# A hybrid convolution and Hyena encoder layer: channel-major inverse transforms, one 31-tap convolution for both groups, stored low parts of weights

## The chip, the cores and the metric

One core of a Trainium2 chip. The metric is the device time of one execution in microseconds. Engines are named as in the profile: PE (TensorE), DVE (VectorE), ACT (ScalarE), POOL (GpSimd), SP (SyncE, which here issues the DMAs).

## What is computed

One encoder layer is applied with the same weights to two groups of tokens, gp (512) and gs (1024), with 1024 features:

```python
h = _ln(x) * (1.0 + scale1) + shift1
proj = jnp.einsum('bld,de->ble', h, w_in)            # 4608 columns, 36 chunks of 128
a = a_val * jax.nn.sigmoid(a_gate)
a = _dwconv(a, conv_dw_w, conv_dw_b)                 # 31 taps, 512 channels
a = jax.nn.silu(_ln(a, conv_ln_g, conv_ln_b))
u = _dwconv(hy_in, hy_short_w, hy_short_b)           # 3 taps, 1536 channels: v, x1, x2
zb = x1 * _fftconv(v, filt[:, 0], hy_skip[0])        # circular, length 2L
zb = x2 * _fftconv(zb, filt[:, 1], hy_skip[1])
m = jax.nn.sigmoid(g_a) * (a @ conv_pw_w) + jax.nn.sigmoid(g_b) * (zb @ hy_out_w)
x = _ln(DEEPNORM_ALPHA * x + gate1 * (m @ w_out), ln1_g[l], ln1_b[l])
f = jnp.square(jax.nn.relu(h2 @ mlp_w1 + mlp_b1)) @ mlp_w2 + mlp_b2
x = _ln(DEEPNORM_ALPHA * x + gate2 * f, ln2_g[l], ln2_b[l])
```

scale, shift and gate come from a product of c with w_ada; filt is the transform of filters that a small MLP with sines makes (`filter_mlp`, `filters`).

## The kernel before

All large products are made of three f32r matmuls. A weight piece (`wpiece`, L209) is loaded into a raw buffer (4 of them), ACT copies it into wt[:, 0] at reduced width (the high part), and DVE subtracts that from raw into wt[:, 1] (the low part); there are six wt buffers. `mm3` (L223) then multiplies high by high, high by low and low by high. Activations are split in the same way into pg tiles. Every instruction on DVE and PE is issued through a `Meter` (L137), whose helper line, 145, stands in the trace for all of them; 202 is the copy in `split`.

The main line runs in this order: w_in(gp), w_in(gs), branches(gp) with the weights w_y, w_out(gp) with the first LayerNorm, the MLP of gp, branches(gs), w_out(gs), and the two products of gs's MLP (`up_seven`, `down_seven`). In the trace these begin at about 38, 270, 905, 960, 1027, 1389, 1502 and 1590 us, up to 2350. w_in takes 36 chunks of 128 columns, two weight pieces each, for 512 tokens at a time; the results go to DRAM as d_a (conv branch), d_h (Hyena) and d_g (gates).

Beside the main line runs side work, in generators that stop at each `yield`: the filters, a Hyena block of 128 channels (`hyena`, four per group), the 31-tap convolution of 128 channels (`conv31`), and its LayerNorm (`conv_ln`). Two lists of them, the lanes, get shares by LANES (L30). After each piece of the main line `pump` (L1623) issues side work as long as the DVE cost counted so far (`vector_cost`, divided by SHARE) is below the PE cost (`tensor_cost`). These costs thus set where side instructions stand between the main ones; each engine then executes its own list in order. Side work of gp that is left when w_in(gs) ends is finished there; that of gs runs on through w_y(gp), w_out(gp) and the MLP of gp.

A Hyena block transforms 128 channels: three-tap convolution (`conv3`), transpose to tokens (`to_tokens`), forward matmuls against tables (fx<-fp,fft), product with the spectrum of the filter (ks, on DVE as sg<-fx,sg), inverse matmuls (`inv_mm`, L355), and sums in `inv_bfly`. It does this twice. The first inverse is token-major (fx<-sg,fft: tables as weights, four matmuls of 128 columns per tile), so that its result meets x1 transposed; the second is channel-major (fx<-fft,sg: the spectrum as weights, two matmuls of 256 columns per tile). In an order's names the tables' tile is fft, PSUM tiles are fx, mm and tr. `conv31` pads one group's 128 channels by 15 on each side and adds 30 shifted products on DVE (cv<-cv,pp, 512 or 1024 columns) to ACT's first.

All DMAs that are named here stand in SP's queue, in order.

Of the kernel before, what the change touches and what calls it, by code (L numbers as in the profile page):

```python
# [25 lines left out]
TAPS = 31  # L26
# [3 lines left out]
LANES = (0.65, 0.35)  # L30
SHARE = 0.88
# [13 lines left out]
STEPS = 3  # L45
PS = (4, 3, 1)
# [14 lines left out]
def fft_tables():  # L61


    n = np.arange(128)[:, None].astype(np.float64)
    k = np.arange(128)[None, :].astype(np.float64)
    h = k[:, :64]
    c0, s0 = np.cos(2 * np.pi * n * h / 128), np.sin(2 * np.pi * n * h / 128)
    s0[:, 0] = (-1.0) ** np.arange(128)
    c8, s8 = np.cos(2 * np.pi * n * (h + 0.5) / 128), np.sin(2 * np.pi * n * (h + 0.5) / 128)
    first = [np.hstack([c0, c8]), np.hstack([c0, -c8]), np.hstack([s0, s8]), np.hstack([s0, -s8])]  # L70
    w = np.ones((64, 1))
    w[0] = 0.5
# [81 lines left out]
def vector_cost(args):  # L154
    return 0.065 + max(free_size(x) for x in args[:2]) / 960.0


def tensor_cost(args):
    return free_size(args[0]) * args[0].shape[0] / 128.0 * (0.00167 if args[2].dtype == F32 else 0.000417)


class Enc:
# [135 lines left out]
    def fwd_mm(self, ti, ev, q, ps):  # L298
# [12 lines left out]
        else:  # L311
            o = self.fft0 + 3 * (ti - 1)
# [42 lines left out]
    def inv_mm(self, g, ys, chan_major):  # L355

        nc, t, f = self.nc, self.T, self.fft
        outs = []
        for pr, y in enumerate(ys):
# [1470 lines left out]
```

## Time and profile before

| | |
|---|---|
| median of 3 runs | 2347.53 us (2347.05 to 2348.93) |
| profiled execution | 2351.76 us, its span 2350.0 us |
| granted TensorE clock, mean | 0.993 |
| busy: PE, DVE, ACT | 2267.9, 1890.1, 920.5 us |
| HBM | 316.16 MB read, 94.43 MB written |

Busy time says how long an engine had an instruction in execution; neighbours overlap by a little, so that counts times durations exceed it. PE's rows are passes: an f32 matmul shows as two rows, an f32r one as one. The span is divided into stretches below, and within a stretch the engine to look at is the one whose instructions the others wait for.

### The profile page before, as it was taken

The numbers are of one execution on the slowest core, as the hardware profiler recorded it, in microseconds if no ns is written. First come the engines' busy times: TensorE is split into PE (matmuls) and PEld (weight loads), VectorE is DVE, ScalarE is ACT, GpSimd is POOL, SyncE is SP. The second block draws the span as 40 slices with busy tenths as digits, with TensorE's granted clock in tenths as the row PEclk, the third lists the DMA queues.
The fourth block names the chain that finished last, engine by engine and source line by source line (L and its number), as shares of the span: only waits on it lengthen the run. The fifth ranks groups of instructions, "written<-read, shape, count | busy, mean of one in ns | idle before, by whom it ended". The sixth has DMA issues, their size and how long they took to land.

```text
span 2350.0 us, 33224 instructions
## 1 busy us (share of the span) xinstructions
PE 2267.9 (97%) x11684; PEld 1882.4 (80%) x11684; DVE 1890.1 (80%) x3662; ACT 920.5 (39%) x1521; POOL 54.3 (2%) x149
## 2 busy tenths in 40 slices
PE   6999999999999999989999999999999999999998
PEld 3878777778878888978888888789887777788886
DVE  5989797786989998895898875965987777577888
ACT  3464522422232223356543344222574444444430
POOL 2210100000000000000000000000000000000000
PEclk9999999999999999999999999999999999999999
DMA  6555434564356646634443344653675666876631
GB/s 246 179 169 175 138 113 163 195 224 159 133 188 203 200 174 215 218 116 144 144 135 99 94 157 154 210 156 109 210 247 188 215 205 214 283 241 215 205 124 71
DMA packets 201068, 412.80 MB, mean 176 GB/s; under 512 B 23321, under 2 KB 33739, under 8 KB 200389
## 3 DMA queue, kind: packets, MB, share of 16 engines
q1 hardware_dynamic: 200069, 409.67, 53.0%
q8 instruction: 92, 1.51, 0.3%
q0 software_dynamic: 832, 1.02, 0.2%
q14 instruction: 75, 0.61, 0.1%
HBM read 316.16 MB, written 94.43 MB: 175 GB/s over the span
## 4 chain that ended last, share of the span: by engine, by line
PE 79%; DVE 9%; DMA 8%; ACT 2%; issue 2%; SPq 1%; DVEq 0%; ACTq 0%
PE mm L145 57%; PE fx L145 19%; PE tr L145 3%; DVE sg L145 2%; DVE pg L145 2%; DVE wt L145 1%; DMA fp<-in_dec_s_dram 1%; DMA sg<-d_xs 1%; DMA fp<-in_w_ada_dram 1%; DVE st L145 1%; DVE fp L145 1%; DMA sg<-in_ffn_w_dram 1%; DMA sg<-ks 1%; DMA raw<-in_w_out_dram 1%; DVE xt L145 1%
## 5 line engine op out<-in xcount | busy, mean ns | idle before, releaser
L145 PE MATMUL mm<-pg,wt 128*128 128x512 f32 (+1 forms) x4776 | 1139.7, 391 | 5.0 <-DVE xt L145 3.6
L145 PEld LDWEIGHTS mm<-pg,wt 128*128 128x128 f32 x4776 | 878.7, 189 | 194.4 <-issue 11.9
L145 PE MATMUL mm<-wt,pg 128*128 128x512 f32 (+1 forms) x2556 | 480.8, 344 | 9.5 <-DVE wt L145 5.0
L145 PEld LDWEIGHTS mm<-wt,pg 128*128 128x128 f32 x2556 | 404.8, 190 | 68.6 <-DVE wt L145 6.8
L202 ACT ACTIVATE wt<-raw 128x512 fp32r<-128x512 f32 x430 | 268.7, 630 | 476.1 <-PE mm L145 375.7
L145 DVE TENSOR_TENSOR wt<-raw,wt 128x512 fp32r<-128x512 f32 x430 | 290.2, 684 | 80.0 <-ACT wt L202 78.1
L145 DVE SCALAR_TENSOR_TENSOR cv<-cv,pp 128x512 f32<-128x512 f32 (+1 forms) x288 | 288.7, 1009 | 7.3 <-ACT cv L853 2.3
L145 PEld LDWEIGHTS fx<-fp,fft 128*128 128x128 f32 x1536 | 177.5, 192 | 20.2 <-issue 15.1
L145 PE MATMUL fx<-fp,fft 128*128 128x128 f32 x1536 | 184.1, 277 | 1.7 <-DVE sm L145 1.1
L145 DVE TENSOR_TENSOR fp<-fp 128x256 f32<-128x256 f32 (+2 forms) x328 | 145.0, 481 | 15.6 <-ACT fp L380 10.2
L145 DVE TENSOR_TENSOR sg<-fx,sg 128x512 f32<-128x512 f32 (+1 forms) x162 | 98.6, 629 | 43.9 <-PE fx L145 27.7
L145 DVE TENSOR_TENSOR pg<-so,pg 128x512 fp32r<-128x512 f32 (+1 forms) x162 | 99.6, 623 | 38.3 <-ACT pg L202 26.9
L145 PE MATMUL fx<-pg,pg 128*128 128x512 f32 x492 | 120.7, 394 | 7.2 <-ACT pg L202 4.3
L145 PEld LDWEIGHTS fx<-pg,pg 128*128 128x128 f32 x492 | 93.5, 190 | 27.5 <-ACT pg L202 4.7
L202 ACT ACTIVATE pg<-so 128x512 fp32r<-128x512 f32 (+1 forms) x127 | 72.1, 575 | 73.9 <-DVE so L145 52.0
L145 PE MATMUL fx<-wt,pg 128*128 128x512 f32 x387 | 95.5, 389 | 0.0
L1260 ACT ACTIVATE so<-so,pp 128x512 f32<-128x512 f32 x62 | 44.4, 719 | 128.8 <-DVE so L145 128.7
L145 DVE TENSOR_TENSOR sg<-sg 128x256 f32<-128x256 f32 (+2 forms) x187 | 82.3, 460 | 6.4 <-ACT sg L890 5.0
L145 PEld LDWEIGHTS fx<-wt,pg 128*128 128x128 f32 x387 | 72.7, 188 | 15.1
L145 PE MATMUL mm<-pg,pg 128*128 128x512 f32 x300 | 73.9, 396 | 5.5 <-DVE xt L145 5.5
L380 ACT ACTIVATE fp<-fx 128x512 f32<-128x512 f32 x48 | 28.7, 598 | 120.6 <-PE fx L145 110.4
L145 DVE TENSOR_TENSOR pg<-pg,pg 128x1024 fp32r<-128x1024 f32 (+1 forms) x45 | 55.0, 1221 | 24.4 <-ACT pg L202 19.6
(175 smaller groups left out, 2221.4 us busy)
## 6 DMA issues: line engine op xcount, KB each, us to landing
raw<-in_mlp_w_dram SPq DMA_DIRECT2D x232, 256.0 KB
raw<-in_w_in_dram SPq DMA_DIRECT2D x144, 256.0 KB
xr<-in_mlp_w_dram SPq DMA_DIRECT2D x104, 256.0 KB
fp<-in_w_ada_dram SPq DMA_DIRECT2D x48, 512.0 KB
pg<-d_p SPq DMA_DIRECT2D x44, 512.0 KB
raw<-in_w_out_dram SPq DMA_DIRECT2D x64, 256.0 KB
d_p<-so SPq DMA_DIRECT2D x64, 256.0 KB
d_g<-so SPq DMA_DIRECT2D x48, 256.0 KB
```

Source lines behind the costliest of these rows:

```text
L145: return f(*args, **kw)
L202: self.nc.scalar.activation(hi, src, AF.Copy)
L380: nc.scalar.activation(outs[-1][:, 4 * (pr % 2):4 * (pr % 2) + 4].rearrange("p (j w) c -> p j w c", j=2), ps, AF.Copy)
L1260: nc.scalar.activation(out, src, AF.Relu, bias=self.pp[:, C_B1 + f:C_B1 + f + 1], scale=1.0)
```

## The change

Three things are changed, and the numbers that place the side work.

- `inv_mm` makes both inverses channel-major with new tables. A real spectrum's inverse is split into the part that is even and the part that is odd about the middle of a block, 64 columns each; two matmuls of 128 columns per tile, instead of four of 128 or two of 256, give the sums, and `unfold` makes the 128 values of a block from them on DVE (a sum, and a difference written backwards). The first inverse's result is therefore channel-major, is multiplied by x1 without a transpose, and is itself transposed for the second transform. The tables fft_sig have 41 blocks of 128 x 128 (2624 KB) where fft_sym had 29 (1856 KB).
- `conv31` takes both groups side by side in one tile (512 + 30 + 1024 columns), in w_in(gs). Its LayerNorm follows for both.
- Chunks 13 to 36 of gp's order in w_in (KEEP = 12) store their low part in DRAM (d_wl); w_in(gs) loads it into the wt buffer in place of the subtraction on DVE.
- LANES, SHARE and the cost functions have other numbers.

```diff
-LANES = (0.65, 0.35)
-SHARE = 0.88
+LANES = (0.4, 0.6)
+SHARE = 1.0
+KEEP = 12
 def vector_cost(args):
-    return 0.065 + max(free_size(x) for x in args[:2]) / 960.0
+    return 0.146 + max(free_size(x) for x in args[:2]) / 960.0
 def tensor_cost(args):
-    return free_size(args[0]) * args[0].shape[0] / 128.0 * (0.00167 if args[2].dtype == F32 else 0.000417)
+    return free_size(args[0]) * args[0].shape[0] / 128.0 * (0.00175 if args[2].dtype == F32 else 0.000443)
-    def inv_mm(self, g, ys, chan_major):
+    def inv_mm(self, g, ys):
...
-                if chan_major:
-                    p = ps[:, j].rearrange("p a b -> p (a b)")
-                    t.matmul(p, yr, f[:, mr[0]:mr[0] + 2].rearrange("p a b -> p (a b)"), start=True, stop=False)
-                    t.matmul(p, yi, f[:, mi[0]:mi[0] + 2].rearrange("p a b -> p (a b)"), start=False, stop=True)
-                else:
-                    for w in range(2):
-                        t.matmul(ps[:, j, w], f[:, mr[w]], yr, start=True, stop=False)
-                        t.matmul(ps[:, j, w], f[:, mi[w]], yi, start=False, stop=True)
+                p = ps[:, j].rearrange("p w (h n) -> p (w h) n", h=2)
+                for n, to in enumerate((slice(0, 3, 2), slice(1, 4, 2)) if ti == 0 else (slice(0, 4, 3), slice(1, 3))):
+                    self.T.matmul(p[:, to], y[:, j, n], f[:, 25 + 2 * ti + n], start=True, stop=True)
...
+    def unfold(self, g, e, mul):
+        v = self.V
+        y = self.fp()
+        a, b = e[:, 0:g.nt, 0:64], e[:, 0:g.nt, 64:128]
+        v.tensor_tensor(y[:, 0:g.nt, 0:64], a, b, op=ALU.add)
+        v.tensor_tensor(y[:, 0:g.nt, 127:63:-1], a, b, op=ALU.subtract)
+        v.tensor_tensor(y[:, 0:g.nt], y[:, 0:g.nt], mul, op=ALU.mult)
+        return y
...
-        dst = self.fp()
-        v.tensor_tensor(dst, e, mul, op=ALU.mult)
-        return dst
+        return self.unfold(g, e, mul)
...
+    def w_in_piece(self, g, c, i):
+        src = self.a["w_in"][c, i]
+        if g.r == 0 or c not in self.keep:
+            return self.wpiece(src, (128, 4, 128))
+        nc = self.nc
+        with self.soon(HW):
+            raw = self.p_raw.tile([128, 4, 128], F32, tag="raw", name="raw")
+            nc.sync.dma_start(raw, src)
+            w = self.p_wt.tile([128, 2, 4, 128], F32R, tag="wt", name="wt")
+            nc.sync.dma_start(w[:, 1].bitcast(F32), self.d_wl[c, i])
+            nc.scalar.activation(w[:, 0], raw, AF.Copy)
+        return w
+    def w_in_pieces(self, g, c):
+        ws = [self.w_in_piece(g, c, i) for i in range(2)]
+        if g.r == 0 and c in self.keep:
+            for i in range(2):
+                self.nc.sync.dma_start(self.d_wl[c, i], ws[i][:, 1].bitcast(F32))
+        return ws
...
+    def hyena(self, g, c):
+        z = blocks(self.conv3(g, c))
+        for o in range(2):
+            x = self.to_tokens(g, z)
+            yield
+            ev, q = self.fwd_bfly(g, x)
+            yield
+            ys = self.conv_core(g, o, c, ev, q)
+            outs = self.inv_mm(g, ys)
+            m = blocks(self.conv3(g, 4 * (o + 1) + c))
+            yield
+            z = self.inv_bfly(g, outs, m)
+            yield
...
-    def conv31(self, g, c):
+    def conv31(self, groups, c):
...
+        for g in groups:
+            nc.gpsimd.memset(u[:, n0:n0 + H], 0.0)
+            nc.gpsimd.memset(u[:, n0 + H + g.L:n0 + 2 * H + g.L], 0.0)
+            nc.sync.dma_start(u[:, n0 + H:n0 + H + g.L], g.d_a[c])
+            at[g] = slice(n0, n0 + g.L)
+            n0 += g.L + 2 * H
+        n -= 2 * H
...
-            v.scalar_tensor_tensor(t, u[:, i:i + L], w(i), t, op0=ALU.mult, op1=ALU.add)
+            v.scalar_tensor_tensor(t, u[:, i:i + n], w(i), t, op0=ALU.mult, op1=ALU.add)
...
-                        if c is not None and c < 4:
-                            self.add_side(self.conv31(g, c), 1)
+                        if c is not None and c < 4 and g is gs:
+                            self.add_side(self.conv31((gp, gs), c), 1)
```

In the order of PE an inverse in w_in(gs) reads as follows before: the token-major kind, and the first rows of the channel-major one.

```order
L145 MATMUL fx<-sg,fft 128x128
L145 MATMUL mm<-pg,wt 128x512 x2
L145 MATMUL fx<-sg,fft 128x128 x7
L145 MATMUL mm<-pg,wt 128x512 x6
L145 MATMUL fx<-sg,fft 128x128 x8
L145 MATMUL fx<-ident,cv 128x128 x4
L145 MATMUL mm<-pg,wt 128x512 x24
L145 MATMUL fx<-fp,fft 128x128 x16
L145 MATMUL mm<-pg,wt 128x512 x6
L145 MATMUL fx<-fft,sg 128x256
L145 MATMUL mm<-pg,wt 128x512
L145 MATMUL fx<-fft,sg 128x256 x3
```

After, one inverse is this:

```order
L158 MATMUL fx<-fp,fft 128x128 x16
L158 MATMUL mm<-pg,wt 128x512 x4
L158 MATMUL fx<-fft,sg 128x2x64
L158 MATMUL mm<-pg,wt 128x512 x4
L158 MATMUL fx<-fft,sg 128x2x64 x2
L158 MATMUL fx<-fft,sg 128x128
L158 MATMUL mm<-pg,wt 128x512 x5
L158 MATMUL fx<-fft,sg 128x2x64
L158 MATMUL fx<-fft,sg 128x128
L158 MATMUL fx<-fft,sg 128x2x64
L158 MATMUL fx<-fft,sg 128x128
```

A tile's four matmuls of 128 columns, or two of 256, have become two of 128, some written as two blocks of 64.

In the order of DVE, at the start of w_out(gp) (pg<-mm,pg is its residual, wt<-raw,wt a weight's low part, the rows with sg, fx and cv are Hyena blocks of gs), the list before is:

```order
L145 TENSOR_TENSOR pg<-mm,pg 128x256
L145 TENSOR_TENSOR sg<-fx,sg 128x512 x2
L145 TENSOR_TENSOR wt<-raw,wt 128x512
L145 TENSOR_TENSOR sg<-sg 128x2x128
L145 TENSOR_TENSOR wt<-raw,wt 128x512 x2
L145 TENSOR_TENSOR pg<-mm,pg 128x256
L145 TENSOR_TENSOR sg<-sg 128x2x128
L145 TENSOR_TENSOR wt<-raw,wt 128x512
L145 TENSOR_TENSOR pg<-mm,pg 128x256
L145 TENSOR_TENSOR sg<-fx,kny 1x128
L145 TENSOR_TENSOR wt<-raw,wt 128x512 x3
L145 TENSOR_TENSOR pg<-mm,pg 128x256
```

And after:

```order
L158 TENSOR_TENSOR pg<-mm,pg 128x256
L158 TENSOR_TENSOR sg<-fx,sg 128x512
L158 SCALAR_TENSOR_TENSOR cv<-cv,pp 128x1024
L158 TENSOR_TENSOR wt<-raw,wt 128x512 x3
L158 TENSOR_TENSOR pg<-mm,pg 128x256
L158 TENSOR_TENSOR wt<-raw,wt 128x512
L158 TENSOR_TENSOR pg<-mm,pg 128x256
L158 TENSOR_TENSOR sg<-sg 128x2x128 x2
L158 TENSOR_TENSOR sg<-fx,sg 128x512 x2
L158 SCALAR_TENSOR_TENSOR cv<-cv,pp 128x1024
L158 TENSOR_TENSOR wt<-raw,wt 128x512 x2
L158 TENSOR_TENSOR pg<-mm,pg 128x256
```

More of gs's Hyena work (the three-tap convolution cv<-cv,pp and products sg<-fx,sg) now stands between the splits of w_out(gp), which themselves are unchanged in number.

In SP's queue in w_in(gs), with what each DMA waits for (DMAHW is the ring slot of an earlier DMA), before:

```order
L215 DMA raw<-in_w_in_dram 128x512 [waits DMAHW3_49,DVE_49]
L215 DMA raw<-in_w_in_dram 128x512 [waits DMAHW4_49,DVE_49]
L688 DMA fp<-in_dec_p_dram 128x1024 [waits DMAHW5_49]
L337 DMA kny<-kny_83 1x128 [waits DMAHW6_49,DVE_49]
L215 DMA raw<-in_w_in_dram 128x512 [waits DMAHW7_49,Activation_49]
L757 DMA d_h_86<-so 128x512 [waits DMAHW0_49,Activation_49]
```

And after, where the low parts are loaded:

```order
L353 DMA sg<-ks_84 128x512 [waits DMAHW6_49]
L749 DMA wt<-d_wl 128x512 [waits DMAHW7_49,PE_49]
L747 DMA raw<-in_w_in_dram 128x512 [waits DMAHW0_49,Activation_49]
L353 DMA sg<-ks_84 128x512 [waits DMAHW1_49]
L749 DMA wt<-d_wl 128x512 [waits DMAHW2_49,PE_49]
L784 DMA d_h_86<-so 128x512 [waits DMAHW3_49,Activation_49]
L747 DMA raw<-in_w_in_dram 128x512 [waits DMAHW4_49,Activation_49]
L350 DMA kny<-kny_83 1x128 [waits DMAHW5_49,DVE_49]
```

A loaded low part waits for PE, whose matmuls last read that wt buffer, and stands in the queue before the raw piece and other DMAs.

## Rows read from the trace of the kernel before

**Rows 1.** The page's first part: busy time, share of the span, instructions of each engine
```profile
PE 2267.9 (97%) x11684; PEld 1882.4 (80%) x11684; DVE 1890.1 (80%) x3662; ACT 920.5 (39%) x1521; POOL 54.3 (2%) x149
```

**Rows 2.** The page's chain that ended last, its shares by engine
```profile
PE 79%; DVE 9%; DMA 8%; ACT 2%; issue 2%; SPq 1%; DVEq 0%; ACTq 0%
```

**Rows 3.** Busy time by stretch; columns in the first line
```profile
core 0: us, PE busy (x) PEld busy (x) DVE busy (x) ACT busy (x) POOL busy (x), PEclk, DMA share, GB/s
38.00:270.00 232.00, 229.87 (x1059) 185.03 (x1060) 191.94 (x371) 114.24 (x193) 30.77 (x46) 1.00 0.54 169
270.00:905.00 635.00, 623.64 (x3444) 510.31 (x3443) 549.30 (x1026) 180.28 (x299) 15.17 (x70) 1.00 0.52 174
905.00:1103.00 198.00, 185.24 (x1128) 163.94 (x1127) 159.21 (x368) 98.22 (x174) 0.28 (x4) 0.97 0.52 168
998.75:1057.50 58.75, 49.77 (x342) 45.15 (x341) 54.59 (x156) 32.55 (x59) 0.00 (x0) 0.91 0.35 116
```

**Rows 4.** Groups of PE: count | busy us, mean ns | idle before, releaser
```profile
L145 PE MATMUL fx<-sg,fft 128*128 128x128 f32 x384 | 47.7, 276 | 2.5 <-DVE sg L145 2.5
L145 PE MATMUL fx<-fft,sg 128*128 128x256 f32 x192 | 46.8, 387 | 1.9 <-DVE sg L145 1.4 <-DVE sm L145 0.3
```

**Rows 5.** Timeline of PE, hyena(gs): start us, length us, merged instructions
```profile
1326.07 3.75 PE L145 MATMUL fx<-sg,fft 128*128 128x128 f32 x32
...
1374.34 3.65 PE L145 MATMUL fx<-fft,sg 128*128 128x256 f32 x16
```

**Rows 6.** Timeline of DVE, w_y(gp)
```profile
917.48 0.68 DVE L145 TENSOR_TENSOR so<-mm,so 128x512 f32<-128x512 f32 x1
918.08 0.68 DVE L145 TENSOR_TENSOR wt<-raw,wt 128x512 fp32r<-128x512 f32 x1
...
920.43 0.41 DVE L145 SCALAR_TENSOR_TENSOR fp<-fp 128x256 f32<-128x256 f32 x1
920.76 0.42 DVE L145 TENSOR_TENSOR fp<-fp 128x256 f32<-128x256 f32 x1
...
924.12 0.48 DVE L145 SCALAR_TENSOR_TENSOR fp<-fp 128x128 f32<-128x128 f32 x2
924.52 0.48 DVE L145 TENSOR_TENSOR fp<-fp 128x128 f32<-128x128 f32 x2
```

**Rows 7.** Groups of DVE, columns as in rows 4
```profile
L145 DVE TENSOR_TENSOR wt<-raw,wt 128x512 fp32r<-128x512 f32 x430 | 290.2, 684 | 80.0 <-ACT wt L202 78.1
L145 DVE SCALAR_TENSOR_TENSOR cv<-cv,pp 128x1024 f32<-128x1024 f32 x144 | 182.4, 1275 | 4.5 <-ACT cv L803 1.4 <-ACT cv L853 1.3 <-issue 0.8
L145 DVE SCALAR_TENSOR_TENSOR cv<-cv,pp 128x512 f32<-128x512 f32 x144 | 107.1, 744 | 2.8 <-ACT cv L853 1.0 <-ACT cv L803 0.9
```

**Rows 8.** Waits of PE, 857 to 1061 us: total us, times, longest us
```profile
PE tr L145 <- ACT pg L515: 7.0, 4, 4.6
```

**Rows 9.** Waits of SP's queue in w_in(gs), 270 to 905 us
```profile
SPq L215 <- DVE wt L145: 68.2, 32, 7.3
```

**Rows 10.** Groups of ACT: one of the table loads, mean ns
```profile
L888 ACT ACT_TABLE_LOAD x1 | 1.3, 1283 | 0.0
```

**Rows 11.** Timeline of PE, w_y(gp) and w_out(gp)
```profile
920.08 20.24 PE L145 MATMUL mm<-pg,wt 128*128 128x512 f32 x88
...
994.20 10.84 PE L145 MATMUL mm<-wt,pg 128*128 128x256 f32 x85
```

**Rows 12.** Waits of DVE, 857 to 1061 us: total us, times, longest us
```profile
DVE wt L145 <- ACT wt L202: 9.2, 8, 2.1
DVE pg L145 <- ACT pg L202: 5.4, 9, 2.2
DVE fp L145 <- DMA fp<-in_dec_s_dram: 3.9, 2, 3.3
DVE pg L145 <- DMA pg<-d_grow: 1.7, 1, 1.7
DVE sg L145 <- DMA sg<-ks: 1.2, 1, 1.2
```

More of the change, by code (lines that the diff above doesn't have):

```diff
@@ L772, in w_in @@
                 for c in ws:
-                    ws[c].append(self.wpiece(self.a["w_in"][c, i], (128, 4, 128)))
+                    ws[c].append(self.w_in_piece(g, c, i))
                     self.w_in_mm(g, c, ws[c], 0, ps[c], i)
@@ L781, in w_in @@
         for cs in first + [[c] for c in order[3:]]:
-            ws = {c: [self.wpiece(self.a["w_in"][c, i], (128, 4, 128)) for i in range(2)] for c in cs}
+            ws = {c: self.w_in_pieces(g, c) for c in cs}
             for tb in range(g.nb):
@@ L837, in hyena @@
-        outs = self.inv_mm(g, ys, True)
-        x2 = self.conv3(g, 8 + c)
-        yield 2.5 * sc
-        zb = self.inv_bfly(g, outs, x2.rearrange("p (a b) -> p a b", b=128))
-        nc.sync.dma_start(g.d_zb[c], zb[:, 0:g.nt].rearrange("p a b -> p (a b)"))
-        yield 8.0 * sc
-    def conv31(self, g, c):
-        nc, v = self.nc, self.V
-        L, H = g.L, TAPS // 2
-        u = self.cv(L + 2 * H)
-        nc.gpsimd.memset(u[:, 0:H], 0.0)
-        nc.gpsimd.memset(u[:, L + H:L + 2 * H], 0.0)
-        nc.sync.dma_start(u[:, H:L + H], g.d_a[c])
+        blocks = lambda t: t.rearrange("p (a b) -> p a b", b=128)
@@ new lines, in hyena @@
+        z = blocks(self.conv3(g, c))
[10 more added lines that the diff above has]
+            yield
+        nc.sync.dma_start(g.d_zb[c], z[:, 0:g.nt].rearrange("p a b -> p (a b)"))
+    def conv31(self, groups, c):
+        nc, v = self.nc, self.V
+        H = TAPS // 2
+        n = sum(g.L + 2 * H for g in groups)
+        u, t = self.cv(n), self.cv(n - 2 * H)
+        at, n0 = {}, 0
+        for g in groups:
[5 more added lines that the diff above has]
+        n -= 2 * H
@@ L856, in conv31 @@
             if i % TAPSTEP == 0:
-                yield 1.0
-        nc.sync.dma_start(g.d_cv[c], t)
+                yield
+        for g in groups:
+            nc.sync.dma_start(g.d_cv[c], t[:, at[g]])
     def conv_ln(self, g, tp):
@@ L1676, in run @@
             self.d_grow = dram.tile([128, 512], F32, tag="d_grow", name="d_grow")
+            self.keep = set(self.chunk_order(gp)[KEEP:])
+            self.d_wl = dram.tile([36, 2, 128, 4, 128], F32, tag="d_wl", name="d_wl")
             self.d_w1 = dram.tile([6, EMB, HID], F32, tag="d_w1", name="d_w1")
@@ L1710, in run @@
                 self.add_side(self.filters(gp))
[L1711 removed]
+                self.add_side(self.load_fft("fft_sig"))
+                pend = []
                 def main_w_in(g, w_in, nxt=None, rest=None):
@@ L1720, in main_w_in @@
                             self.add_side(self.hyena(g, c - 16))
-                        if c is not None and c < 4:
-                            self.add_side(self.conv31(g, c), 1)
-                        if c == 3:
-                            for tp in range(2 * g.nb):
-                                self.add_side(self.conv_ln(g, tp), 1)
+                        if c is not None and c < 4 and g is gs:
+                            self.add_side(self.conv31((gp, gs), c), 1)
+                        if c == 3 and g is gs:
+                            for x in (gp, gs):
+                                for tp in range(2 * x.nb):
+                                    self.add_side(self.conv_ln(x, tp), 1)
+                                if x is gp:
+                                    pend.extend(self.side[1])
                         if prep is not None and n in PREP:
@@ L1732, in run @@
                 main_w_in(gp, w_in, gs)
-                pend = self.side[0] + self.side[1]
+                pend += self.side[0]
                 rest = self.ada_rest()
```

74 lines of the change are left out of this document (27 added, 47 removed).

## The prediction

> **What bounds the kernel now.** I read the totals first, then the chain that ended last, then the busy time by stretch, then the costliest groups and the waits. PE is busy 97% of the span and DVE 80% [rows 1]; 79% of the chain is PE and 9% DVE [rows 2]. So time comes off where matmul work goes, provided that DVE keeps ahead. The stretches show where it does [rows 3]: in both w_in stages PE is idle 2 to 11 us (232 − 229.9 and 635 − 623.6) although DVE has 192 of 232 us and 549 of 635 us to do. From 905 to 1103 us (w_y, w_out and the first mlp_w1 columns of group gp) PE is idle 12.8 us of 198, and the granted clock is 0.97, another 6 us: 19 us lost. At its heart, 998.75 to 1057.5 us, DVE is busy 54.6 of 58.75 us and PE 49.8, and PE's transposes wait for the LayerNorm chain [rows 8]. That is the one place before the end of the side work where DVE is as full as PE, and the change puts work there.
>
> **Inverse transforms on PE.** An f32 matmul is two rows of the trace (two passes), with an f32r one being a single row. Before, 192 matmuls of 128 columns (384 rows) and 96 of 256 columns (192 rows) [rows 4]. Start to start the passes take (3.75 − 0.27)/31 = 0.112 us and (3.65 − 0.38)/15 = 0.218 us [rows 5]: 384 × 0.112 + 192 × 0.218 = 43.0 + 41.9 = 84.9 us. After, 192 matmuls of 128 columns: 384 × 0.112 = 43.0 us. Gain 42 us; by the groups' busy time instead, 47.7 + 46.8 − 47.7 = 47 us. I take **−44 us**, nearer the spacing, because spacing is how PE advances. All of it lies on PE, the bound. Both transposes per channel block stay (x and z1 instead of x and x1): nothing.
>
> **Edits on DVE.** A DVE instruction starts before the one ahead of it has ended: 512 columns last 0.68 us and start 0.60 us apart, 256 columns 0.41 and 0.33, 128 columns 0.28 and 0.20 [rows 6]. So I price DVE at its duration less 0.08 us. Against this speaks the Trainium skill, "VectorE: DVE Perf Modes", section "The DRAIN you can't avoid": the next instruction does not start until the pipe of the one ahead is empty; by full durations the stretch summed below would take DVE some 260 us, and the forecast would be 42 us later. The trace does not agree, at 0.08 us of overlap in each of these pairs.
> - conv31: 120 of 1024 columns at 1.275 − 0.08 and 120 of 512 at 0.744 − 0.08 [rows 7] make 143 + 80 = 223 us. After, 120 of 1566 (512 + 1024 and the 30 pads between): 1.195 + 542 × 0.531/512 = 1.757 us each, 211 us. −12 us.
> - Low parts: 48 subtractions wt<-raw fall away at 0.60 us [rows 6, 7]: −29 us.
> - Unfolding sums and differences: 16 more of 256 columns and 16 more of 512: +15 us.
> Net −26 us on DVE. In the w_in stages, where these lie, PE hardly waits [rows 3], so I cost them at 0 us of time; bounds are 0 and −11, the idle time of the gs stage.
>
> **Queues and ACT.** SP gets 48 stores d_wl<-wt and 48 loads wt<-d_wl of 256 KB. A load waits for PE to free the wt buffer, where SP before had only raw loads waiting for ACT or DVE; queued behind it are the next raw piece, stores of d_h and d_g, and the w_ada pieces, for which PE, DVE's modulation and the next pieces wait. The traffic, 12.6 MB each way, is 81 GB/s over 24/36 of 232 us, on 169 GB/s at a busy share of 0.54, then 30 GB/s over 24/36 of 635 us, on 174 at 0.52 [rows 3]: room enough. SP's raw loads already stand 68 us in 32 waits on DVE's low parts [rows 9] with PE losing 11 us of 635 in all. I take 0; bounds −2 and +10, that idle time once more. The tables of hyena grow by 768 KB, loaded twice: 4.4 us each at 174 GB/s, hidden beside w_in unless a transform is next; 0, at most 9. ACT loads its table 6 times more, 1.28 us each [rows 10]: 8 us on an engine busy 114 of 232 us; 0.
>
> **The moved side work.** conv31(gp) now runs beside conv31(gs), and the gs hyena blocks begin earlier. The order shows the stretch from the filters' multiply that waits for PE (fp<-fx,fp, ahead of w_y) to the split pg<-so,pg of 256 columns that mlp_w1 waits for. In it DVE has 522 instructions: 178 of 512 columns (162 and 16 statistics), 27 of 1024, 167 of 256, 92 of 128, 58 of two columns. At 0.60, 1.18, 0.33, 0.20 and about 0.1 us [rows 6, 7] that is 107 + 32 + 55 + 18 + 6 = **218 us**. PE has 245 f32 matmuls (490 passes at 0.112), 509 f32r of 256 columns at (10.84 − 0.29)/84 = 0.126, 192 of 512 at (20.24 − 0.39)/87 = 0.228, and 60 transposes at 0.112 [rows 5, 11]: 55 + 64 + 44 + 7 = **170 us**. DVE can't begin before PE has passed the first mark, and PE can't pass the second before DVE has: 48 us without PE work, whatever lies between. In before, the tightest like pair (pg<-mm,pg of w_out to the same split) has 158 on DVE, 60 us, and PE 52 us: 8 us. The other 11 of the 19 us are latencies. Of these I keep 7 (d_grow, ks and part of the waits of pg on ACT's copy [rows 12]), since DVE now has other work to put into the rest: 48 + 7 = 55 against 19, **+36 us**. Bounds: 0 if that work fits into DVE's idle time there (198 − 159 = 39 us [rows 3], by which the 36 would vanish), and +68 if all that idle time stays on top (48 + 39 − 19). I take the middle because the longest of these waits is for ACT's copy wt [rows 12], and that copy waits for PE to free a buffer: with DVE late, the buffers are free before it asks.
>
> **Sum.** −44 + 36 = −8 us. The profiled execution took 2351.8 us (span 2350.0); 2343.8 us on its scale. The median of the runs is 4.2 us below it, so **2339 us**.
>
> **Rivals.**
> 1. *The whole gain stays.* DVE fills its own 39 idle us and the stretch costs no more than now: 2347.5 − 44 = 2303 us. For: PE waited there mostly for one LayerNorm chain [rows 8]. Against: DVE executes in order, and 218 against 170 us leaves no choice unless instructions are cheaper than their rows. 0.13.
> 2. *Slower: DVE's stretch with its latencies on top.* At w_out(gp) the order puts hyena's sg<-fx and conv3 between the splits. If the waits on ACT's wt and pg, decay tables and d_grow, 9.2 + 5.4 + 3.9 + 1.7 = 20 us [rows 12], all come on top, the loss is 48 + 20 = 68, +49 against now: 2347.5 − 44 + 49 = 2352 us; with all 39 idle us 2371. It decides from 15 us on top (48 + 15 = 44 + 19). For: those waits are there today. Against: a late DVE finds its inputs ready. 0.20.
> 3. *SP's queue stands behind wt<-d_wl.* The gs stage loses 10 more: 2349 us. For: a new wait on PE at the head of an in-order queue, 48 times. Against: six wt buffers and raw loads that already wait [rows 9]. 0.06.
> 4. *The matmuls do not get cheaper.* Were a pass with two blocks of 64 columns as dear as one of 256, 384 × 0.218 = 84 us, the gain would be 1 us: 2347.5 − 1 + 36 = 2382 us. The rows know only whole blocks [rows 5], at cost by column. 0.03.
> 5. *The clock.* Around PE's gaps between 998.75 and 1057.5 us the granted clock averages 0.91, between its levels of 2.4 and 1.2 GHz [rows 3]; at 0.91 PE's 170 us become 187, still under DVE's 218, so the sum is untouched. At the lower level throughout they become 340: 340 − 170 − 19 = +151, 2454 us. The Trainium skill, "TensorE: Matmul & The Clock Gate", section "HAM oscillation", says that gaps between bursts make the clock fall again and again, and so speaks for this. The trace agrees in kind, at 0.91 and not lower. 0.03.
>
> **How the numbers follow.** A measurement of this kernel can tell about 0.2%, 4.7 us, from no change. My forecast has 0.55, with its own range 2328 to 2349: faster 0.40, same 0.13, slower 0.02. Rival 1: faster 0.13. Rival 2: same 0.02, slower 0.18. Rival 3: half and half. Rivals 4 and 5: slower 0.06. Together faster 0.53, same 0.18, slower 0.29. The range, 2310 to 2362, leaves out the far half of rival 1 and what lies above rival 2's lower price.
>
> **What would show it.** The inverse group on PE at 384 rows and about 48 us; DVE's conv group at 120 instructions of 1.84 us; 382 subtractions wt<-raw. PE's idle time between the start of w_y(gp) and the first mlp columns should rise from 13 to about 50 us, with DVE there above 90% busy and PE waiting for DVE's so, pg and wt. PE should wait no longer in w_in(gs). If PE's idle time in that stretch stays under 25 us, the order's sum was wrong and rival 1 holds; if w_in(gs) has over 20 us of PE waits, it was the queue.

## The result and the profile after

| | before | changed |
|---|---|---|
| median (lowest to highest) | 2347.29 us (2346.20 to 2348.93, 4 runs) | 2364.39 us (2361.93 to 2364.96, 4 runs) |
| ratio | | 1.0069, 95% interval 1.0055 to 1.0083 |
| profiled execution, span | 2351.76, 2350.0 us | 2364.44, 2362.6 us |
| mean granted clock | 0.993 | 0.984 |

The change made the kernel 17 us slower; 2339 us was forecast. The totals and the chain of the changed kernel, to set beside [rows 1, 2]:

```profile
PE 2247.5 (95%) x11492; PEld 1859.5 (79%) x11492; DVE 1869.4 (79%) x3526; ACT 929.0 (39%) x1523; POOL 54.0 (2%) x149
...
PE 77%; DVE 11%; DMA 7%; issue 2%; ACT 2%; SPq 1%; DVEq 0%; ACTq 0%
```

PE has 20 us less busy time in a longer span, and DVE 21 us less. More of the chain is DVE (11% for 9%) and less is PE. The profiled execution of the kernel before stood 4.5 us above its median, that of the changed kernel at its median: between the two profiles below there are 12.7 us, between the medians 17.

The edits themselves came out as priced. The groups of the changed kernel (count | busy us, mean ns | idle before), to set beside [rows 4, 7]:

```profile
L158 PE MATMUL fx<-fft,sg 128*128 128x128 f32 x384 | 53.4, 276 | 1.9 <-DVE sg L158 1.8
```

```profile
L158 DVE TENSOR_TENSOR wt<-raw,wt 128x512 fp32r<-128x512 f32 x382 | 257.6, 685 | 85.4 <-ACT wt L215 83.7
L158 DVE SCALAR_TENSOR_TENSOR cv<-cv,pp 128x1566 f32<-128x1566 f32 x120 | 220.6, 1841 | 4.3 <-ACT cv L879 3.7
```

The inverses are 384 passes where they were 576, and the joint conv31 is 120 instructions of 1.84 us, as worked out. 48 subtractions are gone. The inverse's 53.4 us of busy time is above the 43 us of its spacing: its timeline shows groups of eight passes in 1.05 to 1.08 us, 0.112 us apart as before, but they are cut into more pieces between other matmuls, and a piece counts its last pass at full length (0.27 us), which the next piece overlaps.

The time was lost by stretch. Here each kernel is cut at the same places of its own program: the first matmul of w_in(gp), w_in(gs) and w_y(gp), the one that first reads the 13th weight piece of mlp_w1, and the first of w_y(gs). Busy time by stretch, columns in the first line, of the kernel before:

```profile
core 0: us, PE busy (x) PEld busy (x) DVE busy (x) ACT busy (x) POOL busy (x), PEclk, DMA share, GB/s
37.80:264.10 226.30, 224.15 (x1029) 180.77 (x1029) 186.64 (x361) 108.70 (x184) 30.98 (x46) 1.00 0.54 171
264.10:905.70 641.60, 630.24 (x3482) 515.45 (x3481) 555.20 (x1036) 186.71 (x309) 15.17 (x70) 1.00 0.52 174
905.70:1103.40 197.70, 184.94 (x1123) 163.58 (x1122) 159.23 (x369) 97.53 (x173) 0.28 (x4) 0.97 0.52 167
1103.40:1502.60 399.20, 392.34 (x2049) 332.56 (x2048) 328.60 (x718) 164.19 (x277) 0.94 (x14) 1.00 0.43 138
```

And of the changed kernel:

```profile
38.50:274.10 235.60, 233.89 (x1072) 187.24 (x1073) 197.88 (x402) 120.89 (x205) 39.67 (x54) 1.00 0.63 203
274.10:892.70 618.60, 598.18 (x3235) 479.84 (x3234) 499.16 (x843) 195.92 (x320) 5.77 (x61) 1.00 0.61 204
892.70:1174.30 281.60, 243.75 (x1543) 220.93 (x1541) 257.56 (x605) 113.14 (x194) 1.45 (x18) 0.91 0.49 163
1174.30:1513.20 338.90, 333.83 (x1643) 281.04 (x1643) 253.32 (x496) 134.49 (x225) 0.13 (x2) 1.00 0.42 132
```

A stretch does not hold the same side work in both, so its length alone says little. The table sets against it PE's own work there: all its passes in the order, priced at 0.112 us (f32, 128 columns), 0.227 us (f32r, 512) and 0.118 us (f32r, 256). What is left is idle time, lowered clock, and small gaps. One price is too low: the passes of w_ada, which fill 32 output rows, come out of this table at about 0.11 us each, and take about 0.22 in the trace (28 of them 6.20 us in w_in(gp)). So some 13 us of what is left in w_in(gs) and 3 in w_in(gp) are work; they are the same in both kernels, and the differences do not change.

| stretch | length | PE's work | left, before | length | PE's work | left, changed | difference |
|---|---|---|---|---|---|---|---|
| w_in(gp) | 226.3 | 219 | 7 | 235.6 | 226 | 10 | +2 |
| w_in(gs) | 641.6 | 599 | 43 | 618.6 | 562 | 57 | +14 |
| w_y(gp) to mlp_w1's 13th piece | 197.7 | 173 | 25 | 281.6 | 216 | 66 | +41 |
| rest of mlp(gp) | 399.2 | 389 | 10 | 338.9 | 333 | 6 | −4 |

PE's work falls by 43 us over the four, and what is left grows by 53; behind them the two kernels differ by under 3 us. The third stretch is DVE's, as its line shows: 257.6 us busy of 281.6, PE idle 37.9 us and the granted clock 0.91. PE's idle time is 38 of the 66 us left; the other 28 are passes that took longer than their price (244 us for 216), where before they were 12 of 25, at a granted clock of 0.97. At the heart of the stretch, in w_y, DVE has no idle time at all (57.00 of 57.00 us, PE 45.23):

```profile
947.00:1004.00 57.00, 45.23 (x258) 39.41 (x257) 57.00 (x146) 15.60 (x24) 0.13 (x2) 0.85 0.36 112
```

PE's waits in the third stretch (total us, times, longest us):

```profile
PE mm L158 <- DVE pg L158: 10.7, 4, 4.3
PE fx L158 <- DVE fp L158: 7.9, 6, 4.0
PE mm L158 <- DVE so L158: 7.7, 1, 7.7
PE fx L158 <- DVE sg L158: 5.0, 3, 3.4
PE tr L158 <- ACT pg L522: 4.6, 2, 4.0
```

Three of the longest, in the timeline (start us, length us, and in brackets the idle time ahead and who ended it):

```profile
960.47 1.94 PE L158 MATMUL fx<-ident,fp 128*128 128x128 f32 x8 [4.03 <-DVE fp L158]
...
994.31 5.45 PE L158 MATMUL mm<-pg,wt 128*128 128x512 f32 x12 [7.74 <-DVE so L158]
...
1041.92 8.40 PE L158 MATMUL mm<-wt,pg 128*128 128x256 f32 x48 [4.29 <-DVE pg L158]
```

PE stands 7.74 us for DVE's so in w_y and some 4 us each for the transpose of z1 (fx<-ident,fp) and for pg. In w_in(gs), where 0 us was forecast, PE is idle 20.4 us for 11.4, and the waits are small and many (before, in the same stretch: w_ada 2.8, DVE's fp 3.2, d_t 0.9 us):

```profile
PE tr L158 <- DMA fp<-in_w_ada_dram: 7.5, 7, 2.9
PE fx L158 <- DVE fp L158: 7.0, 5, 3.0
PE fx L158 <- DMA sg<-d_t: 4.0, 3, 2.0
```

### The profile page after: what moved, and what is told of

Its sections match the earlier page's. It is cut to its first block, busy times and chain, and to the rows that moved or that the text cites. A ratio compares the mean times of both kernels' runs of the same rounds, so it can differ in the third digit from the quotient of the medians.

```text
span 2362.6 us, 32799 instructions
## 1 busy us (share of the span) xinstructions
PE 2247.5 (95%) x11492; PEld 1859.5 (79%) x11492; DVE 1869.4 (79%) x3526; ACT 929.0 (39%) x1523; POOL 54.0 (2%) x149
## 4 chain that ended last, share of the span: by engine, by line
PE 77%; DVE 11%; DMA 7%; issue 2%; ACT 2%; SPq 1%; DVEq 0%; ACTq 0%
PE mm L158 56%; PE fx L158 17%; DVE fp L158 3%; PE tr L158 3%; DVE pg L158 2%; DVE sg L158 2%; DMA fp<-in_w_ada_dram 1%; DMA sg<-d_xs 1%; DVE wt L158 1%; DMA fp<-in_dec_s_dram 1%; DVE so L158 1%; DVE st L158 1%; DMA sg<-ks 1%; DVE xt L158 1%; DMA fft<-in_fft_sig_dram 0%
## 5 line engine op out<-in xcount | busy, mean ns | idle before, releaser
L158 PEld LDWEIGHTS mm<-wt,pg 128*128 128x128 f32 x2556 | 410.8, 194 | 76.3 <-DVE pg L158 15.4
L215 ACT ACTIVATE wt<-raw 128x512 fp32r<-128x512 f32 x382 | 239.0, 629 | 415.3 <-PE mm L158 305.7
L158 DVE TENSOR_TENSOR wt<-raw,wt 128x512 fp32r<-128x512 f32 x382 | 257.6, 685 | 85.4 <-ACT wt L215 83.7
L158 DVE SCALAR_TENSOR_TENSOR cv<-cv,pp 128x1566 f32<-128x1566 f32 (+2 forms) x168 | 268.1, 1604 | 9.9 <-ACT cv L830 4.7
L158 DVE TENSOR_TENSOR fp<-fp 128x256 f32<-128x256 f32 (+2 forms) x352 | 154.6, 476 | 20.1 <-ACT fp L381 10.4
L786 ACT ACTIVATE so<-mm 128x512 f32<-128x512 f32 x48 | 28.8, 599 | 116.2 <-PE mm L158 71.3
L158 PEld LDWEIGHTS mm<-pg,pg 128*128 128x128 f32 x300 | 55.2, 188 | 21.7 <-DVE xt L158 10.5
```

The lines of the kernel that those rows point to most:

```text
L158: return f(*args, **kw)
L215: self.nc.scalar.activation(hi, src, AF.Copy)
L786: nc.scalar.activation(o, ps, AF.Sigmoid)
```

## The experiments

Each was run together with the kernel before on the same chip; medians, with the ratio to before and its interval. The runs came in four groups, on three chips, and the kernel before took 2345.9 to 2347.6 us beside them. "DVE's excess by the order" is the sum that the prediction made for one stretch, taken over the whole program: for each pair of places where DVE waits for PE and later PE for DVE, DVE's work between them less PE's, at the largest. It is 11 us in the kernel before and 55 in the changed one. In the changed kernel the pair is the prediction's own; of the 7 us above its 48, some 4 come from pricing PE's 256-column passes at 0.118 us and not at 0.126. The columns "left" come from one profiled execution each. The run without low parts in w_out(gp) tells how far such a one can be trusted: its instructions in w_in(gs) are those of the changed kernel, and it has 65 us left there for 57. Differences of up to some 8 us in that column show nothing by themselves.

| run | median us | ratio (interval) | excess by the order | left, w_in(gs) | left, w_y(gp) to mlp |
|---|---|---|---|---|---|
| before | 2347.3 | | 11 | 43 | 25 |
| changed | 2364.4 | 1.0069 (1.0055 to 1.0083) | 55 | 57 | 66 |
| old inverse | 2406.1 | 1.0242 (1.0219 to 1.0266) | 48 | 66 | 63 |
| no stored low parts | 2353.3 | 1.0027 (1.0014 to 1.0041) | 42 | 51 | 55 |
| before + inverse + low parts | 2356.6 | 1.0034 (1.0021 to 1.0047) | 18 | 52 | 42 |
| no low parts in w_out(gp) | 2349.1 | 1.0007 (0.9992 to 1.0022) | 36 | 65 | 48 |
| LANES 0.55, 0.45 | 2347.3 | 1.0008 (0.9993 to 1.0022) | 30 | 56 | 50 |
| LANES 0.55, 0.45, no low parts | 2364.9 | 1.0089 (1.0072 to 1.0106) | 22 | 75 | 42 |
| before + inverse | 2364.7 | 1.0087 (1.0070 to 1.0104) | 27 | 40 | 39 |
| before + low parts | 2381.4 | 1.0161 (1.0133 to 1.0188) | 17 | 55 | 37 |
| low parts by POOL's queue | 2365.5 | 1.0100 (1.0062 to 1.0138) | 52 | 58 | 67 |
| before + conv31 + numbers | 2402.5 | 1.0245 (1.0219 to 1.0271) | 32 | 67 | 56 |
| before + inverse, SHARE 0.92 | 2341.5 | 0.9978 (0.9967 to 0.9990) | 19 | 46 | 42 |
| before + transfers alone | 2356.6 | 1.0045 (1.0030 to 1.0060) | 11 | 45 | 22 |
| before + numbers | 2453.0 | 1.0451 (1.0433 to 1.0468) | 55 | 55 | 118 |
| before + inverse, SHARE 0.90 | 2333.0 | 0.9942 (0.9927 to 0.9957) | 19 | 36 | 36 |

The expectations name theories by letters. A: the loss is DVE's excess in the third stretch, the prediction's 48 us and the latencies on top. B: it is the new loads and stores, by SP's in-order queue. C: the inverse's matmuls are no cheaper. D: the new inverse's longer chain on DVE delays what follows it. E: it is the transfers' traffic (E1), or where the lists put the work (E2).

**The old inverse in the changed kernel.** `inv_mm`, `unfold`, `hyena` and the tables go back to those of before, all else stays.

```diff
...
-        return self.unfold(g, e, mul)
+        dst = self.fp()
+        v.tensor_tensor(dst, e, mul, op=ALU.mult)
+        return dst
```

> The changed kernel with the old inverses (token-major and channel-major, no unfolding) and everything else of the change. Theory A (the new inverse saves PE its 42 us, and DVE's excess of work between w_y(gp) and mlp(gp) gives them back): PE has 43 us more to do and DVE's excess shrinks by 7 us, so about 36 us slower than the changed kernel, 2400 us. Theory C (the new matmuls are not cheaper on PE): within 5 us of the changed kernel, 2364 us.

42 us slower than the changed kernel. The new inverse does take PE's work away, at about its price, and the rival on dear matmuls falls.

**No stored low parts.**

```diff
-            self.keep = set(self.chunk_order(gp)[KEEP:])
+            self.keep = set()
```

> The changed kernel without stored low parts: DVE subtracts them again in w_in(gs), 29 us more on DVE, and 96 DMAs fewer. Theory A: DVE's excess in the stretch is 42 instead of 55 us by its order, so about 13 us faster, 2351 us. Theory B (the loads that wait for PE hold up SP's queue, and that is what the change lost): at least 17 us faster, with PE's waits for the w_ada loads in w_in(gs) back from 7.5 to about 3 us. If the 29 us of DVE work counted in w_in(gs): slower, 2375 us or more.

11 us faster than the changed kernel: 29 us more of subtraction on DVE cost nothing here, as priced. (With other lanes, further below, the same edit loses 18 us.) It does not tell A from B: some 8 us came back in the w_in stages and 10 in the third stretch, the former no more than two executions of the same instructions differed by.

**Before, with inverse and stored low parts.** conv31, its places and the numbers are those of before; the two edits shown under "The inverse alone" and "Stored low parts alone" are made together.

> The kernel before with the new inverses and the stored low parts, but its own conv31 (each group apart, when its own w_in has made its input) and its own numbers for placing the side work. Theory A: DVE's excess over PE in the stretch falls to some 18 us (11 in the kernel before), PE keeps 43 us less work: about 37 us faster than before, 2311 us. Theories B and C: no faster than before, 2347 us or more, because the queue or the matmuls are as in the changed kernel.

9 us slower than before. The order's excess was wrong by 46 us as a forecast; the time is left in w_in(gs) (+9), in w_y(gp) to mlp (+17) and in later stretches. So the place of conv31 alone is not the cause, and later runs took the parts one by one.

**No low parts in w_out(gp).**

```diff
-                    ws = [self.wpiece(self.a["w_out"][qc, d], (128, 2, 256)) for d in range(KD // 2)]
+                    ws = [self.w_hi(self.a["w_out"][qc, d], (128, 2, 256)) if g.r == 0 else self.wpiece(self.a["w_out"][qc, d], (128, 2, 256)) for d in range(KD // 2)]
...
-                                self.mm3(po, p[:, 0, k], p[:, 1, k], w[:, 0, d % 2], w[:, 1, d % 2], d == 0, d == KD - 1)
+                                self.mm3(po, p[:, 0, k], p[:, 1, k], w[:, 0, d % 2], w[:, int(g.r > 0), d % 2], d == 0, d == KD - 1)
...
```

> The changed kernel without the 32 subtractions of low parts in w_out(gp); the matmul that reads the low part reads the high part again, so PE and the DMAs do the same work (the output lacks that correction). Theory A (DVE is the bound there): DVE has 19 us less in the stretch, so about 19 us faster, 2345 us. If the stretch is held by latencies (LayerNorm chain, ACT) or by PE's lowered clock: within 5 us of the changed kernel.

15 us faster than the changed kernel. Its third stretch (columns as above):

```profile
900.50:1164.30 263.80, 236.17 (x1541) 213.58 (x1541) 239.37 (x573) 112.42 (x194) 1.40 (x18) 0.95 0.53 174
```

It is 17.8 us shorter with PE's work the same and 18.2 us less on DVE: an almost even trade, so DVE bounds that stretch. PE's idle time fell and its granted clock rose together (37.9 to 27.6 us; 0.91 to 0.95). No time beyond the 18 us came back with the clock, so no cost of the lowered clock by itself can be seen here; nor is it excluded, since no run changed the clock alone.

**Other lanes.** One line of the changed kernel.

```diff
-LANES = (0.4, 0.6)
+LANES = (0.55, 0.45)
```

> The changed kernel with one line changed, LANES (0.55, 0.45) for (0.4, 0.6): conv31, the DVE work that needs no PE, is spread further towards the end of w_in(gs), and filters and Hyena blocks come earlier. All counts are the same. Theory A (the time is lost where DVE's work in the order exceeds PE's): that excess is 30 instead of 55 us, so about 25 us faster than the changed kernel, 2339 us. If the amount of work and not its place decides (theory B, or a fixed cost of the new inverse): within 5 us of the changed kernel, 2364 us.

17 us faster with the same instructions: a change of placement alone takes back the whole loss against the kernel before. The third stretch gave 16 of it. In w_in(gs), where conv31 now ends at 855 us for 745, 56 us are left, as in the changed kernel.

**Other lanes, no stored low parts.** Both lines together, in the changed kernel.

```diff
-LANES = (0.4, 0.6)
+LANES = (0.55, 0.45)
...
-            self.keep = set(self.chunk_order(gp)[KEEP:])
+            self.keep = set()
```

> As the last one (LANES (0.55, 0.45)) and without stored low parts. Theory A: excess 22 instead of 55 us, about 33 us faster than the changed kernel, 2331 us, and faster than the kernel before. Theory B (the queue): both effects add, 2328 us or less, of which the waits for w_ada loads are 5. If the 29 us of subtraction bind: 2360 us.

A miss: as slow as the changed kernel. The third stretch did come down to 42 us, but w_in(gs) rose to 75. With the subtractions back, side work that must be done before w_y(gp) piles up at the end of w_in(gs):

```profile
900.00:940.20 40.20, 17.59 (x99) 13.13 (x97) 29.50 (x101) 13.42 (x25) 0.13 (x2) 0.70 0.32 100
```

PE is busy 17.6 of those 40.2 us, and 15 us of its waits there are for ACT's cv in the LayerNorm behind conv31. The order's excess weighs DVE against PE alone and does not show a pile that goes through ACT.

**The inverse alone.** The kernel before, with `inv_mm`, `unfold`, `hyena` and the tables of the change.

```diff
-    def inv_mm(self, g, ys, chan_major):
+    def inv_mm(self, g, ys):
...
-        dst = self.fp()
-        v.tensor_tensor(dst, e, mul, op=ALU.mult)
-        return dst
+        return self.unfold(g, e, mul)
```

> The kernel before with the new inverses alone. Theory A by its order: PE 43 us less, DVE's excess 27 instead of 11 us, so 27 us faster than before, 2320 us. Theory D (formed after the kernel with inverses and stored low parts, which came out 9 us slower than before where the order gave 37 us faster: the first inverse now must go through DVE's sums and a transpose on PE before the second transform can start, and PE stands behind that transpose and the transforms): PE's waits for DVE rise at each block and the gain is gone, 2345 us or more, with PE waiting for fx<-ident,fp and fx<-fp,fft.

18 us slower than before, as theory D said; w_in(gs) is as good as before (40 us left), but the third stretch has 39 and the MLP of gp 40 us left where it had 10. PE's waits in that MLP:

```profile
PE mm L158 <- ACT pg L215: 6.8, 1, 6.8
PE fx L158 <- DVE sg L158: 6.2, 3, 3.4
PE mm L158 <- DVE pg L158: 5.7, 4, 2.9
```

Two of them are waits of the main line (ACT's copy and pg). The Hyena wait among them is for sg, the product ahead of an inverse; DVE's fp, for which the transposes that D names would wait, is not among PE's waits there, and ACT's copy of a transposed block, for which the transforms wait, comes to 1.7 us. That speaks against D's mechanism.

**Stored low parts alone.** The kernel before, with `w_in_piece` and `w_in_pieces`.

```diff
-            ws = {c: [self.wpiece(self.a["w_in"][c, i], (128, 4, 128)) for i in range(2)] for c in cs}
+            ws = {c: self.w_in_pieces(g, c) for c in cs}
...
+            self.keep = set(self.chunk_order(gp)[12:])
```

> The kernel before with the stored low parts alone. Theory A: PE's work is the same and DVE's excess 17 instead of 11 us: 6 us slower at most, 2347 to 2353 us, since the 29 us that DVE saves lie where PE does not wait. Theory B (the queue): the loads that wait for PE hold up the w_ada and raw loads, 10 us slower or more, with PE's waits for w_ada at 7 us or more (2.8 before). If DVE binds in w_in(gs): up to 29 us faster.

34 us slower, far outside A: 5 us in w_in(gp), at a DMA share of 0.69 for 0.54, 12 in w_in(gs), 12 in the third stretch. PE's waits for w_ada are 7.0 us, as B expected.

**Low parts by POOL's queue.**

```diff
-            nc.sync.dma_start(w[:, 1].bitcast(F32), self.d_wl[c, i])
+            nc.gpsimd.dma_start(w[:, 1].bitcast(F32), self.d_wl[c, i])
...
-                self.nc.sync.dma_start(self.d_wl[c, i], ws[i][:, 1].bitcast(F32))
+                self.nc.gpsimd.dma_start(self.d_wl[c, i], ws[i][:, 1].bitcast(F32))
```

> The changed kernel with the stores and loads of the low parts issued by POOL's queue instead of SP's. The same transfers, and a load that waits for PE no longer stands ahead of the w_ada, raw and d_t loads. Theory B (SP's queue is what the stored low parts cost, 8 to 18 us in the two w_in stages in the pairs so far): 6 us or more faster than the changed kernel, PE's waits for w_ada in w_in(gs) from 7.5 back to about 3 us. Theory E (the traffic or the moved order costs it, not the queue): within 4 us of the changed kernel, 2364 us, w_ada waits unchanged.

No faster, and PE still waits for w_ada:

```profile
PE tr L158 <- DMA fp<-in_w_ada_dram: 7.3, 7, 1.8
```

So it is not that a waiting load stands ahead of others in SP's queue. The Trainium skill, "DMA: Bandwidth & Descriptors", section "Issuing engines are not separate DMA queues", says that transfers issued by different engines end up on the same 16 DMA engines and that another issuing engine saves only issue time. This run agrees, at 1.0100 for 1.0069.

**conv31 and numbers.** The kernel before, with the joint `conv31`, LANES, SHARE and costs of the change (the numbers are shown under "Numbers alone").

```diff
-                        if c is not None and c < 4:
-                            self.add_side(self.conv31(g, c), 1)
+                        if c is not None and c < 4 and g is gs:
+                            self.add_side(self.conv31((gp, gs), c), 1)
```

> The kernel before with the joint conv31 and the new numbers alone: old inverses, no stored low parts. Theory A by its order: DVE's excess 32 instead of 11 us: 21 us slower than before, 2367 us; with the stored low parts (the run with the old inverse, 2406 us) the order gave 47. If joint conv31 costs nothing by itself: 2347 us.

55 us slower, where the order gave 21. In w_in(gs) 67 us are left for 43, without any stored low part.

**The inverse alone, SHARE 0.92.**

```diff
-SHARE = 0.88
+SHARE = 0.92
```

> The run with the new inverses alone, with SHARE 0.92 for 0.88: the same instructions, side work issued a little earlier, so that the Hyena blocks of gs end well before the MLP of gp does. Theory A (place of DVE's work): the 40 us that PE stood in the MLP of gp and the 20 in w_y and w_out of gs go back to some 15 and 9 as before, excess in the order 19 instead of 27 us: 2335 us, faster than before. Theory D (the new inverse's longer chain costs PE at every block, wherever it stands): within 8 us of that run, 2365 us.

23 us faster than with 0.88, and some 5 us faster than before. Theory D falls: the same chain, a little earlier, costs nothing like it. The MLP of gp has 19 us left instead of 40 and w_y and w_out of gs 9 instead of 20.

**Transfers alone.** The kernel before, with the stores, and loads into a tile that nothing reads.

```diff
...
+                if g.r == 0:
+                    self.nc.sync.dma_start(self.d_wl[c, i], ws[i][:, 1].bitcast(F32))
+                else:
+                    self.nc.sync.dma_start(self.p_dump.tile([128, 4, 128], F32, tag="dump", name="dump"), self.d_wl[c, i])
```

> The kernel before with the 48 stores of low parts in w_in(gp) and 48 loads of them in w_in(gs) into a tile that nothing reads; DVE subtracts all low parts as before. Theory E1 (the traffic of 12.6 MB each way, not the queue and not the missing subtractions, costs what the stored low parts cost in the w_in stages): PE's waits for w_ada in w_in(gs) 7 us (2.8 before), 5 to 17 us slower than before, 2352 to 2364 us. Theory E2 (it is the placement that the changed costs bring): 2347 us, w_ada waits at 3.

9 us slower, of which 7 in w_in(gp), where the stores are:

```profile
38.70:272.10 233.40, 227.24 (x1029) 183.03 (x1029) 187.87 (x361) 108.98 (x184) 31.00 (x46) 0.99 0.77 251
```

Its DMA share there is 0.77 and PE is idle 6.2 us for 2.2; left are 14 us for 7. But the run is not the one that was meant. Since its loads wait for no buffer that PE reads, they run ahead, and 30 of the 48 are issued in w_in(gp) already (SP's issues in that stage):

```profile
dump<-d_wl SPq DMA_DIRECT2D x30, 256.0 KB
```

The last is issued at 306.5 us. So the 7 us belong to 48 stores and 30 loads together; the stores without the loads cost 5 us there in the run with stored low parts alone. And the loads as the changed kernel has them, spread over w_in(gs), are not tested: that the w_ada wait is 1.9 us here says nothing about them. PE waits 3.7 to 9.4 us for w_ada in the kernels with stored low parts, 0.9 to 4.2 us in those without. SP's queue is not the reason; whether the traffic is stays open.

**Numbers alone.** The kernel before with four lines changed.

```diff
-LANES = (0.65, 0.35)
-SHARE = 0.88
+LANES = (0.4, 0.6)
+SHARE = 1.0
...
-    return 0.065 + max(free_size(x) for x in args[:2]) / 960.0
+    return 0.146 + max(free_size(x) for x in args[:2]) / 960.0
-    return free_size(args[0]) * args[0].shape[0] / 128.0 * (0.00167 if args[2].dtype == F32 else 0.000417)
+    return free_size(args[0]) * args[0].shape[0] / 128.0 * (0.00175 if args[2].dtype == F32 else 0.000443)
```

> The kernel before with the new LANES, SHARE and cost functions alone; every instruction is the same, only placed otherwise. Theory A by its order: DVE's excess 55 instead of 11 us, 44 us slower than before, 2391 us; then the 56 us of the run with the joint conv31 and the numbers are mostly the numbers. If the joint conv31 itself costs them: within 10 us of before.

105 us slower, with not one instruction of PE or DVE added. Its third stretch:

```profile
836.30:1246.70 410.40, 327.62 (x2125) 297.39 (x2126) 333.34 (x794) 130.32 (x222) 2.62 (x24) 0.91 0.48 159
```

It takes 410 us, with PE idle 83 us and DVE also idle 77: what is left, 118 us, is more than the order's excess, because a list in which DVE's work is bunched waits for DMAs and ACT too (22.3 us for the decay tables, 17.0 for ACT's wt). In w_in(gs) 55 us are left for 43, with none of the three edits made. The constants say what moved: for 512 columns on DVE the new one gives 0.679 us, the length in [rows 6], the old one 0.598, the spacing; with SHARE both come to 0.68, but 128 columns rise from 0.225 to 0.279 us, and a 512-column pass of PE from 0.214 to 0.227. Which of the lines costs most was not taken apart.

**The inverse alone, SHARE 0.90.**

```diff
-SHARE = 0.88
+SHARE = 0.90
```

> As the run with the new inverses and SHARE 0.92, with 0.90. Theory A: excess by its order 19 us as there, so within 8 us of it, 2334 to 2349 us. Theory D (a fixed cost of the longer chain): between that run and the one with 0.88, 2350 us or more.

14.6 us faster than before: the fastest of the versions. Its first four stretches, cut as above:

```profile
39.10:266.50 227.40, 224.25 (x1031) 181.08 (x1031) 190.21 (x368) 109.25 (x185) 31.05 (x47) 1.00 0.53 169
266.50:868.70 602.20, 594.64 (x3250) 481.86 (x3247) 530.70 (x981) 179.88 (x296) 14.44 (x68) 1.00 0.53 178
868.70:1086.90 218.20, 196.29 (x1234) 176.36 (x1234) 179.91 (x424) 98.09 (x173) 0.53 (x4) 0.95 0.52 174
1086.90:1481.80 394.90, 379.91 (x1977) 319.92 (x1977) 337.30 (x735) 170.69 (x288) 1.06 (x16) 0.99 0.44 141
```

36 us are left in w_in(gs) (43 before), 36 in the third stretch (25), 25 in the MLP of gp (10). Of the 43 us that PE saves, the stretches give back some 20.

## Why the prediction was wrong

The forecast was 2339 us, range 2310 to 2362, and the changed kernel takes 2364. By the prediction's own steps:

- **Inverse transforms, −44 us: right.** PE's work fell by 43 us, and with the old inverse the changed kernel is 42 us slower.
- **Edits on DVE, −26 us and 0 us of time: the prices were right, the 0 depends on the order.** With the subtractions back, the changed kernel lost no time to 29 us more of them, but with LANES 0.55, 0.45 it lost 18 us. As for the price of a DVE instruction, the Trainium skill speaks less against it than the prediction says: "VectorE: DVE Perf Modes", section "The DRAIN you can't avoid", goes on to say that an instruction which is not held (the page's word) starts earlier.
- **Queues, 0 with bounds of −2 and +10, and the w_in stages as a whole at 0: this step failed.** They lost 16 us (2 in gp, 14 in gs), and PE's idle time in w_in(gs) went from 11.4 to 20.4 us, past the 20 that I had named as the sign of the queue. But the rival's mechanism, SP's queue, is refuted: the same loads from POOL's queue cost as much. What the runs show in its place is two things. The place of the side work costs time in w_in(gs) as well, which I had asked of DVE's total there and not of the order: the new numbers alone leave 55 us for 43, and with the joint conv31 67, both without any stored low part. And the stores are not free: 5 us in w_in(gp) in the kernel before, some 2 in the changed one; I had called 81 GB/s more "room enough" from a share of 0.54. How the 14 us in w_in(gs) divide between placement and stored low parts stays open. At its end (765 to 893 us), when conv31 is done, DVE is busy 77 of 128 us while PE is idle 10 us, mostly for the filters' products; that the filters lack something to run beside is argued only, and the run that moved conv31 to a later end left as much.
- **The moved side work, +36 us: nearly right.** The stretch lost 41 (66 left for 25). That DVE bounds it is shown by the run without low parts in w_out(gp), 18 us less on both sides. The term was 48 + 7 against 19; it measured 66 against 25.
- **The rest of mlp(gp), not costed:** −4 us.
- **The step from the profiled execution to the median, −4.2 us: right.** It puts the −8 us of the sum on the median of the kernel before. The stretches above show 4 us less than the loss between medians, because the profile of the kernel before is one of its slower executions.

In sum −43 + 16 + 41 − 4 is +10 us, with some 2 us behind the four stretches and at the start 12.6 us of span, and 17 us between medians, where −8 was forecast for both. Rival 2 is what happened, in its place and for its reason, but its price of 2352 us lacked the w_in stages. Rivals 3 and 4 are refuted, rival 1 did not occur. Of rival 5 the rows show a granted clock of 0.91 over 281.6 us, for 0.97 in the same stretch before; that it added to the time was not separated.

Deeper than the missing 16 us is what I took the change to be. I priced three edits and read the new numbers only through the order they made. The runs show that the numbers alone cost the kernel before 105 us, that one line of them is worth 17 us in the changed kernel, and that two values of SHARE stand 32 us apart for the inverse (2364.7 and 2333.0). No part was a gain at the places it was given by itself, and the inverse became one when its side work was placed anew.

## What to carry to other kernels

When an order is made by costs and shares, an edit that takes work from the bound engine can be worth nothing until the other engine's work is placed anew: sweep those numbers with each edit, and judge the edit by the best of them. Summing each engine's work between two points where they wait for each other is a good test for a stretch that a second engine will bound (41 us measured for 36), but it is a lower bound: across the runs some 10 to 25 us more were left there, and 63 where that work was bunched. As a forecast of a whole kernel's time it missed by 28 to 62 us in six of the twelve runs it was used for, each time on the slow side. A single profiled execution can stand 4 to 8 us off its kernel's median; compare stretches of two kernels with that in mind.

## What had not been expected

- A change of LANES, SHARE and three cost constants, with every instruction the same, took the kernel from 2347.6 to 2453.0 us.
- 48 stores of 256 KB lengthened w_in(gp) of the kernel before by 5 us, at a DMA share of 0.69 for 0.54, and with 30 loads beside them by 7 us, at 0.77.
- Taking 29 us of work off DVE in a stage where it is 87% busy made the kernel before 34 us slower. Transfers of the same size cost 9; that the rest is the order that came with the edit is likely from the other runs, but was not separated.
